# A fused two-block kernel: the RWKV stage with each head in its own half of the partitions

## The chip, the cores and the metric

The program runs on one core of one Trainium2 chip. A core has a matrix engine (TensorE, PE in the profile; its weight loads are PEld), three engines that work on vectors (VectorE or DVE, ScalarE or ACT, GpSimd or POOL), a queue engine that issues transfers (SyncE, SP), an on-chip memory of 128 partitions (SBUF), accumulators of 128 partitions (PSUM) and 16 DMA engines. The metric is the time of one execution on the device, in microseconds (us); less is better.

## The reference

Two transformer blocks follow each other over 512 tokens of 1024 channels, in float32: RWKV-7 in both directions beside neighbourhood attention, gated and projected; a mixture of experts; a second block of Hyena, gated linear attention and gated delta rule, and an MLP. The change touches the RWKV part, which has 8 heads of 64 channels:

```
r, k, v, ... = split(token_shift(h @ w_in))
kk = k * k_k;  kk = kk * rsqrt(sum(kk * kk, per head) + 1e-12)
step:  sa = S @ (-kk);  S = S * w + outer(sa, kk * a) + outer(v, k);  y = S @ r      # forward and backward in time
y = (y_f + y_b - mean) * rsqrt(var + eps) * lnx_g + lnx_b                            # per head
out = (y + sum(r * (k_f + k_b) * r_k, per head) * v) * g
```

## The kernel before, in words

The recurrence is computed in 8 chunks of 64 tokens. Two heads make a pair (128 partitions); 4 pairs times 2 directions are 8 units. For a unit, `dir_prep` (L487) makes decay factors (tiles cps to frho, fbet, falp), the scaled keys BK, the scaled queries EO, transposed copies (BKT, SV, VU) and the products of keys with keys (lps, L568), masked on DVE. `inverse` (L641) inverts the unit triangular matrix of each chunk and head: its 16x16 diagonal blocks go to DRAM and back so that each block lies on a partition of its own (L662, L664), are inverted by 15 steps of substitution on DVE (L671, L672), come back (L675, L677) and are combined by four rounds of 16 products of 64x64 (L692), which give TQ (L710). `scan` (L577) then goes through the chunks: xp (L585), copied to X, up = TQ X (L597), copied, sp (L603), and the next state on DVE (L605). The outputs yp (L613, L614) use states and values of all chunks. For the backward direction a group norm follows (L620 to L635), and `pair_prep` (L414) makes what a pair's two directions share.

In the code before, the two terms of a sum (state and value, say) are added by a product over all 128 partitions: the head's own half holds state and queries, the other half values and masked key products. So xp, sp and half of yp are products of 128 rows by 64 columns of the array, while up, the other half of yp and the inverse's products are 64 by 64.

A generator per activity writes the program down in turn (`weave`, L326): the next unit's preparation and inverse beside the present unit's scan, and all of this (weight 800) beside a filler (weight 170): gates and modulation rows (mps, L1227, from w_modb), then the projections of neighbourhood attention (`na_proj`: gpt, L319 to L321, then eight blocks gps with sums of squares, L735 to L741). A projection block is 24 products of 128x128 by 512 columns (gps, L288 to L290) with weights split on ACT and DVE (wh, wl). A scheduler of the framework then fixes the order on each engine when the program is built: it prefers what was written first among what it believes ready. At run time every engine goes through its list in order. A float32 product is two records on PE, one in float32r or a transpose is one.

Of the kernel before, what the change touches and what calls it, by code (L numbers as in the profile page):

```python
# [10 lines left out]
F32 = mybir.dt.float32  # L11
F32R = mybir.dt.float32r
I32 = mybir.dt.int32
AF = mybir.ActivationFunctionType
OP = mybir.AluOpType
# [10 lines left out]
# ---------------------------------------------------------------- constants (shapes alone)  # L26
def const_tables():
# [7 lines left out]
    c["bd16"] = np.tile(((s_[:, None] // 16) == (s_[None, :] // 16)).astype(np.float32), (2, 1))  # L35
# [41 lines left out]
def bias_table(rpb):  # L77
    """rpb [8, 15, 31] laid out per head and kind of column block as [128 queries, 256 keys], -1e30 out of the window"""
# [12 lines left out]
def blocks(w, cols):  # L91
    """w [1024, n] -> [len(cols), 128, 8, 128]: column blocks (-1: zeros), rows k*128 + p at [p, k]"""
# [9 lines left out]
def w2_cols():  # L102
    """column blocks of the second input projection: name -> list of 128 columns"""
# [41 lines left out]
def pad_heads(a):  # L145
    """[..., 192] -> [..., 256]: each head's 48 columns at a multiple of 64"""
# [27 lines left out]
class Tags:  # L174
    """a pool whose tags go by other names"""
# [8 lines left out]
class K:  # L184
# [8 lines left out]
    def view(self, tags, **kw):  # L193
        """the same kernel for a stream of its own: other PSUM tags, other pools"""
# [6 lines left out]
    # ---- constants  # L201
# [10 lines left out]
    def cvec(self, name, ap, n, pool=None):  # L212
        """A per-channel vector of n values as [128, n/128] columns."""
# [9 lines left out]
    # ---- 1/sqrt of a small tile, in place of x  # L223
# [20 lines left out]
        # the squares themselves go where the transposed parts will  # L244
# [27 lines left out]
    # ---- weights: raw load, exact split  # L272
# [2020 lines left out]
```

## Time and profile before

| | us |
|---|---|
| three runs | 2248.74, 2264.35, 2252.16 |
| median | 2252.16 |
| profiled execution, first to last instruction | 2259.9 |
| of these, until the last product of the RWKV stage's filler (L741) | 662.7 |
| PE busy / DVE busy / ACT busy / POOL busy, whole span | 2016.9 / 1253.3 / 725.8 / 314.7 |
| mean granted TensorE clock | 0.926 |

The profiled execution gives no time beside its span; the span is 7.7 us (0.3%) over the median and within the spread of the three runs. A busy PE is not a PE at its peak. Matmul records overlap, since they are pipelined, so what a product costs is read from start to start and not from its printed duration.

### The profile page before, as it was taken

How to read it: one execution, taken by the hardware profiler on the slowest of the kernel's cores; microseconds unless marked ns; L12 is line 12 of the kernel's file. 1: busy time of each engine (PE TensorE's matmuls, PEld its weight loads, DVE VectorE, ACT ScalarE, POOL GpSimd, SP SyncE). 2: the span in 40 equal slices, each digit the busy share in tenths (PEclk: the TensorE clock that was granted, in tenths of full speed). 3: DMA queues.
4: the chain of work that ended last, by engine and by line, in shares of the span. 5: the costliest groups of instructions: out<-in, count | busy, mean ns of one | idle time of the engine just before them, and what ended most of it. 6: DMA issues, size and time to landing. Idle time of an engine off the chain costs nothing. (4 is left out here: it accounts for less than half of the span.)

```text
span 2259.9 us, 34926 instructions
## 1 busy us (share of the span) xinstructions
PE 2016.9 (89%) x13608; PEld 1439.2 (64%) x13608; DVE 1253.3 (55%) x2742; ACT 725.8 (32%) x1422; POOL 314.7 (14%) x358
## 2 busy tenths in 40 slices
PE   7999999989968888989999487899989788999997
PEld 5666666657745675444534265676757477899897
DVE  4776777864326545554461487667447375433433
ACT  4332333222215433121322365423224125312321
POOL 0222222220110201102000031210001050000000
PEclk9999999998969998999999798998679899999998
DMA  5232221263267428897786532333113432222222
GB/s 150 99 107 80 66 88 55 76 204 114 92 209 230 143 87 297 294 346 244 297 309 225 192 112 86 101 113 106 38 47 132 162 112 94 93 94 94 94 94 75
DMA packets 183017, 319.25 MB, mean 141 GB/s; under 512 B 77896, under 2 KB 99160, under 8 KB 182842
## 3 DMA queue, kind: packets, MB, share of 16 engines
q1 hardware_dynamic: 175354, 303.28, 40.2%
q0 software_dynamic: 4608, 8.40, 1.1%
q10 hardware_dynamic: 2880, 5.24, 0.8%
q8 instruction: 109, 1.79, 0.3%
q14 instruction: 66, 0.54, 0.1%
HBM read 281.80 MB, written 43.44 MB: 144 GB/s over the span
## 5 line engine op out<-in xcount | busy, mean ns | idle before, releaser
L283 DVE TENSOR_TENSOR wl<-wraw,wh 128x1024 fp32r<-128x1024 f32 (+2 forms) x215 | 227.9, 1062 | 199.8 <-ACT wh L282 199.2
L282 ACT ACTIVATE wh<-wraw 128x1024 fp32r<-128x1024 f32 (+2 forms) x233 | 195.6, 844 | 274.2 <-PE gpt L321 145.1
L288 PE MATMUL gps<-hh,wh 128*128 128x512 f32 x568 | 236.3, 417 | 0.6 <-ACT wh L282 0.4
L290 PE MATMUL gps<-hl,wh 128*128 128x512 f32 x568 | 231.8, 409 | 0.0
L289 PE MATMUL gps<-hh,wl 128*128 128x512 f32 x568 | 231.6, 409 | 0.0
L1173 PE MATMUL hps<-w,xT 128*64 128x512 f32 x512 | 142.5, 610 | 3.4 <-DMA w<-in_w_moe 3.3
L320 PE MATMUL gpt<-wl,mh 128*128 128x256 f32 x512 | 142.9, 279 | 0.0
L319 PE MATMUL gpt<-wh,mh 128*128 128x256 f32 x512 | 142.9, 279 | 0.0
L321 PE MATMUL gpt<-wh,ml 128*128 128x256 f32 x512 | 142.9, 279 | 0.0
L288 PEld LDWEIGHTS gps<-hh,wh 128*128 128x128 f32 x568 | 108.4, 191 | 30.6 <-ACT st L765 1.4
L289 PEld LDWEIGHTS gps<-hh,wl 128*128 128x128 f32 x568 | 108.4, 191 | 24.2 <-issue 1.0
L290 PEld LDWEIGHTS gps<-hl,wh 128*128 128x128 f32 x568 | 107.9, 190 | 24.2 <-issue 0.7
L1999 POOL TENSOR_TENSOR x<-x,xev 128x512 f32<-128x512 f32 x36 | 49.9, 1392 | 407.9 <-DVE xev L1997 358.6
L289 PE MATMUL gps<-lhh,wl 128*128 128x512 f32 x232 | 96.4, 417 | 10.2 <-DVE wl L283 8.6
L288 PE MATMUL gps<-lhh,wh 128*128 128x512 f32 x232 | 96.2, 417 | 7.6 <-ACT cpad L1265 4.6
L319 PEld LDWEIGHTS gpt<-wh,mh 128*128 128x128 f32 x512 | 96.2, 188 | 0.1
L320 PEld LDWEIGHTS gpt<-wl,mh 128*128 128x128 f32 x512 | 96.2, 188 | 0.1
L321 PEld LDWEIGHTS gpt<-wh,ml 128*128 128x128 f32 x512 | 96.2, 188 | 0.0
L290 PE MATMUL gps<-lhl,wh 128*128 128x512 f32 x232 | 94.7, 410 | 0.2 <-DVE lhl L270 0.2
L1173 PEld LDWEIGHTS hps<-w,xT 128*64 128x64 f32 x512 | 37.1, 138 | 66.3 <-issue 51.2
L2015 DVE TENSOR_TENSOR uld<-uld 128x512 f32<-128x512 f32 x32 | 22.2, 692 | 88.1 <-ACT uld L2014 88.1
L319 PE MATMUL gpt<-wh,uh 128*128 128x256 f32 x224 | 66.0, 295 | 5.6 <-ACT wh L282 2.4
(1164 smaller groups left out, 4437.7 us busy)
## 6 DMA issues: line engine op xcount, KB each, us to landing
w<-in_w_moe SPq DMA_DIRECT2D x192, 512.0 KB
wraw<-in_w_modb SPq DMA_DIRECT2D x48, 512.0 KB
wraw<-in_w_in_2b SPq DMA_DIRECT2D x41, 512.0 KB
wraw<-in_w_inb SPq DMA_DIRECT2D x39, 512.0 KB
wraw<-in_w_mlp1b SPq DMA_DIRECT2D x32, 512.0 KB
wraw<-in_w_mlp2b SPq DMA_DIRECT2D x32, 512.0 KB
gd<-st SPq DMA_DIRECT2D x16, 256.0 KB
bm<-in_c_bias SPq DMA_DIRECT2D x16, 256.0 KB
```

The lines of the kernel that those rows point to most:

```text
L282: nc.scalar.activation(wh, raw[:, o:o + g], AF.Copy)
L283: self.we.tensor_sub(wl, raw[:, o:o + g], wh)
L288: nc.tensor.matmul(ps, wh, hh, start=first, stop=False)
L289: nc.tensor.matmul(ps, wl, hh, start=False, stop=False)
L290: nc.tensor.matmul(ps, wh, hl, start=False, stop=last)
L319: nc.tensor.matmul(ps, hh[:, g, sl], wh[:, k], start=f, stop=False, skip_group_check=True)
L320: nc.tensor.matmul(ps, hh[:, g, sl], wl[:, k], start=False, stop=False, skip_group_check=True)
L321: nc.tensor.matmul(ps, hl[:, g, sl], wh[:, k], start=False, stop=l, skip_group_check=True)
L1173: nc.tensor.matmul(ps[q], xT[:, 4 * kh + k, q], self.parts[h][:, 512 * (k - 2 * c):512 * (k - 2 * c) + 512], start=kh == 0 and k == 0, sto ...
L1999: (nc.gpsimd if last is None or cb < 3 else nc.vector).tensor_add(o, o, t)
L2015: nc.vector.tensor_mul(f, f, f)
```

## The change

Each head now stays in its own half of the partitions for both operands of every product, and the two terms of a sum are two products that accumulate in PSUM. BK becomes BE and KA, EO becomes AR with the masked products apart in PB and PK, and SV and VU become S, U and V. Elementwise operations that ran once per half run once over 128 partitions; the state scale no longer needs POOL; the copy of up is one ACT operation. Beta, kappa and values are transposed by products of 64x64 with the identity. Both norms take their root on [128, 4, 2] values and are spread again by ACT and four products (`over_norm`) in place of a root and a reciprocal over [128, 512]. The inverse gets its diagonal blocks by a mask of their own (nd16) straight from PSUM and its other blocks from PB. The gated delta rule's inverse keeps its operations (`in_parts`). In the diff, docstrings and comments are left out.

```diff
     blk[:64, :64] = 1.0
     blk[64:, 64:] = 1.0
     c["blk"] = blk
-    c["bd16"] = np.tile(((s_[:, None] // 16) == (s_[None, :] // 16)).astype(np.float32), (2, 1))
+    up, same = s_[:, None] < s_[None, :], lambda n: (s_[:, None] // n) == (s_[None, :] // n)
+    two = lambda a: np.tile(a.astype(np.float32), (2, 1))
+    c["bd16"] = two(same(16))
+    c["nd16"] = two(up & same(16))
+    far = up & ~same(16)
+    c["pm"] = two(np.concatenate([far, s_[:, None] <= s_[None, :]], 1))
...
-                TQ, = yield from self.inverse([U["N"]], d)
+                TQ, = yield from self.inverse([(U["Nd"], lambda q, P=U["PB"]: P[q, :, 0, :])], d)
...
+    def over_norm(self, sq, pool, eps, scale, name):
+        nc, C = self.nc, self.C
+        ps = self.ps.tile([128, 4, 2], F32, name=name + "s", tag="p", bufs=2)
+        for tt in range(4):
+            nc.tensor.matmul(ps[:, tt], sq[:, tt * 128:(tt + 1) * 128], C["blk"][:, ::64], start=True, stop=True)
+        r = pool.tile([128, 4, 2], F32, name=name + "r")
+        nc.scalar.activation(r, ps, AF.Sqrt, bias=eps, scale=scale)
+        nc.vector.reciprocal(r, r)
+        R = pool.tile([128, 4, 2, 64], F32, name=name + "b", tag="rs")
+        nc.scalar.activation(R, r[:, :, :, None].to_broadcast([128, 4, 2, 64]), AF.Copy)
+        ps = self.ps.tile([128, 512], F32, name=name + "p", tag="p", bufs=2)
+        for tt in range(4):
+            nc.tensor.matmul(ps[:, tt * 128:(tt + 1) * 128], R[:, tt].rearrange("p h c -> p (h c)"), C["ident"], start=True, stop=True)
+        return ps
...
         kk = pt.tile([128, T], F32, name="kk")
         sq = pt.tile([128, T], F32, name="sq", tag="sq")
         nc.scalar.activation(sq, kS, AF.Square, scale=self.kkv[:, hp:hp + 1])
...
+        ps = self.over_norm(sq, pt, self.eps12, 1.0, "kn")
...
         frho, fbet, falp = fac
-        BK = pt.tile([128, 8, 2, 64], F32, name="BK")
+        BE, KA = [pt.tile([128, 8, 64], F32, name=n) for n in ("BE", "KA")]
         b = self.rt.tile([128, T], F32, name="bb", tag="sq")
+        tm = lambda ap: nat(ap).rearrange("p (c t) -> p c t", t=64)
         nc.vector.scalar_tensor_tensor(b, a, 1.0, kk, op0=OP.add, op1=OP.mult)
...
+        nc.vector.scalar_tensor_tensor(BE, tm(b), 0.5, fbet, op0=OP.mult, op1=OP.mult)
+        nc.gpsimd.tensor_mul(KA, tm(kd), fbet)
+        AR = rp.tile([128, 8, 2, 64], F32, name=f"AR{d}")
+        nc.vector.tensor_mul(AR[:, :, 0, :], tm(kk), falp)
+        nc.vector.tensor_mul(AR[:, :, 1, :], tm(rS), frho)
         Dc = rp.tile([128, 8], F32, name=f"Dc{d}")
         nc.vector.reciprocal(Dc[:, :7], falp[:, 1:, 0])
         nc.vector.tensor_mul(Dc[:, :7], Dc[:, :7], frho[:, :7, 63])
...
         if d:
-            vr = self.rt.tile([128, T + 64], F32, name="vr", tag="rs")
-            nc.vector.tensor_copy(vr[:, 64:], vS[:, 64:][:, ::-1])
-            nc.gpsimd.memset(vr[:, :64], 0.0)
+            vr = self.rt.tile([128, T], F32, name="vr", tag="rs")
+            nc.vector.tensor_copy(vr, vS[:, ::-1])
         else:
             vr = vS
...
+        tok = []
+        for n, x in (("BT", BE), ("KT", KA), ("V", vr.rearrange("p (c t) -> p c t", t=64))):
+            ps = ps_.tile([128, 8, 64], F32, name="tps", tag="p", bufs=2)
+            for c in range(8):
+                for q in hq:
+                    nc.tensor.matmul(ps[q, c], x[q, c], C["ident"][q, q], start=True, stop=True)
+            o = rp.tile([128, 8, 64], F32, name=f"{n}{d}")
+            nc.scalar.activation(o, ps, AF.Copy)
+            tok.append(o)
+        Nd = pt.tile([128, 8, 64], F32, name=f"Nd{d}")
+        PB, PK = [rp.tile([128, 8, 2, 64], F32, name=f"{n}{d}") for n in ("PB", "PK")]
         for g in range(2):
-            for h in range(2):
-                q, o = slice(64 * h, 64 * h + 64), slice(64 - 64 * h, 128 - 64 * h)
+            sl = slice(4 * g, 4 * g + 4)
+            for x, o, m in ((BE, PB, "pm"), (KA, PK, "mask")):
                 ps = ps_.tile([128, 4, 128], F32, name="lps", tag="p", bufs=2)
                 for c in range(4):
...
+                    for q in hq:
+                        nc.tensor.matmul(ps[q, c, :], x[q, 4 * g + c], AR[q, 4 * g + c].rearrange("p a t -> p (a t)"), start=True, stop=True)
+                if x is BE:
+                    nc.vector.tensor_mul(Nd[:, sl], ps[:, :, :64], C["nd16"][:, None, :].to_broadcast([128, 4, 64]))
+                nc.vector.tensor_mul(o[:, sl].rearrange("p c a t -> p c (a t)"), ps, C[m][:, None, :].to_broadcast([128, 4, 128]))
+        return dict(Nd=Nd, PB=PB, PK=PK, AR=AR, Dc=Dc, tok=tok)
...
         nc, C, ps_, pt = self.nc, self.C, self.ps, self.rd
-        EO, SV, VU, BKT, Dc = U["EO"], U["SV"], U["VU"], U["BKT"], U["Dc"]
+        AR, PB, PK, Dc = U["AR"], U["PB"], U["PK"], U["Dc"]
+        BT, KT, V = U["tok"]
         hq = [slice(64 * h, 64 * h + 64) for h in range(2)]
+        S = self.rp.tile([128, 8, 64], F32, name=f"S{d}")
+        Us = self.rp.tile([128, 8, 64], F32, name=f"U{d}")
         for c in range(8):
             xp = ps_.tile([128, 64], F32, name="xp", tag="s", bufs=2)
-            for h, q in enumerate(hq):
-                nc.tensor.matmul(xp[q], EO[h][:, c, 0, :], SV[h][:, c, :], start=True, stop=True)
+            for q in hq:
+                nc.tensor.matmul(xp[q], PK[q, c, 0, :], V[q, c, :], start=True, stop=c == 0)
+            if c:
+                for q in hq:
+                    nc.tensor.matmul(xp[q], AR[q, c, 0, :], S[q, c, :], start=False, stop=True)
             X = pt.tile([128, 64], F32, name="X", bufs=2)
             nc.vector.tensor_copy(X, xp)
-            if c < 7:
+            if 0 < c < 7:
                 SD = pt.tile([128, 64], F32, name="SD", bufs=2)
-                for h, q in enumerate(hq):
-                    if h:
-                        nc.gpsimd.tensor_scalar(SD[q], SV[h][q, c, :], Dc[q, c:c + 1], None, op0=OP.mult)
-                    else:
-                        nc.scalar.activation(SD[q], SV[h][q, c, :], AF.Copy, scale=Dc[q, c:c + 1])
+                nc.scalar.activation(SD, S[:, c, :], AF.Copy, scale=Dc[:, c:c + 1])
             up = ps_.tile([128, 64], F32, name="up", tag="s", bufs=2)
-            for h, q in enumerate(hq):
+            for q in hq:
                 nc.tensor.matmul(up[q], TQ[q, c, :], X[q], start=True, stop=True)
-            nc.scalar.activation(VU[0][hq[0], c, :], up[hq[0]], AF.Copy)
-            nc.vector.tensor_copy(VU[1][hq[1], c, :], up[hq[1]])
+            nc.scalar.activation(Us[:, c, :], up, AF.Copy)
             if c < 7:
                 sp = ps_.tile([128, 64], F32, name="sp", tag="s", bufs=2)
-                for h, q in enumerate(hq):
-                    nc.tensor.matmul(sp[q], BKT[:, c, h, :], VU[h][:, c, :], start=True, stop=True)
-                for h, q in enumerate(hq):
-                    nc.vector.scalar_tensor_tensor(SV[h][q, c + 1, :], sp[q], Dc[q, c:c + 1], SD[q], op0=OP.mult, op1=OP.add)
+                for q in hq:
+                    nc.tensor.matmul(sp[q], KT[q, c, :], V[q, c, :], start=True, stop=False)
+                for q in hq:
+                    nc.tensor.matmul(sp[q], BT[q, c, :], Us[q, c, :], start=False, stop=True)
+                if c:
+                    nc.vector.scalar_tensor_tensor(S[:, c + 1, :], sp, Dc[:, c:c + 1], SD, op0=OP.mult, op1=OP.add)
+                else:
+                    nc.vector.tensor_scalar(S[:, 1, :], sp, Dc[:, 0:1], None, op0=OP.mult)
             yield 2.5
         if d == 0:
             self.y = self.ry.tile([128, T], F32, name="y")
         y = self.y
         yp = ps_.tile([128, 8, 64], F32, name="yp", tag="i", bufs=2)
         for c in range(8):
-            for h, q in enumerate(hq):
-                nc.tensor.matmul(yp[q, c, :], SV[h][:, c, :], EO[h][:, c, 1, :], start=True, stop=False)
-                nc.tensor.matmul(yp[q, c, :], VU[h][q, c, :], U["MB"][q, c, :], start=False, stop=True)
+            for q in hq:
+                nc.tensor.matmul(yp[q, c, :], V[q, c, :], PK[q, c, 1, :], start=True, stop=False)
+            if c:
+                for q in hq:
+                    nc.tensor.matmul(yp[q, c, :], S[q, c, :], AR[q, c, 1, :], start=False, stop=False)
+            for q in hq:
+                nc.tensor.matmul(yp[q, c, :], Us[q, c, :], PB[q, c, 1, :], start=False, stop=True)
         ypf = yp.rearrange("p c t -> p (c t)")
         if d == 0:
             nc.scalar.activation(y, ypf, AF.Copy)
         nc.vector.tensor_add(y, ypf[:, ::-1], y)
...
-        ps = ps_.tile([128, 512], F32, name="vps", tag="p", bufs=2)
-        nc.tensor.matmul(ps, C["blk"], sq, start=True, stop=True)
-        nc.scalar.activation(sq, ps, AF.Sqrt, bias=self.epsgn, scale=1.0 / 64)
-        nc.vector.reciprocal(sq, sq)
-        nc.vector.scalar_tensor_tensor(y, y, self.lng[:, hp:hp + 1], sq, op0=OP.mult, op1=OP.mult)
+        ps = self.over_norm(sq, pt, self.epsgn, 1.0 / 64, "yn")
+        nc.vector.scalar_tensor_tensor(y, y, self.lng[:, hp:hp + 1], ps, op0=OP.mult, op1=OP.mult)
         nc.vector.scalar_tensor_tensor(y, y, self.lnb[:, hp:hp + 1], bo, op0=OP.add, op1=OP.add)
         nc.gpsimd.tensor_mul(y, y, P["gt"])
         nc.sync.dma_start(self.yad[hp * 128:(hp + 1) * 128, :], y)
...
         fb = self.rib
         F = pt.tile([128, nz, 8, 16], F32, name="F16", bufs=fb)
...
+        for z, (Nd, _) in enumerate(Ns):
+            nc.vector.tensor_reduce(F[:, z], Nd.rearrange("p u (b t) -> p u t b", b=4), axis=AX.X, op=OP.add)
...
+                    nc.tensor.matmul(ps[q, u, :], lhs(q)[:, u, :], rhs[q, u, :], start=True, stop=True)
         Z, W = [], list(Qd)
         for z in range(nz):
-            ps = mm(No[z], Vd[z])
-            Z.append(pt.tile([128, 8, 64], F32, name="Z", tag="zw", bufs=2 * nz))
+            ps = mm(Ns[z][1], Vd[z])
+            Z.append(pt.tile([128, 8, 64], F32, name="Z", tag="zw", bufs=2))
             nc.scalar.activation(Z[z], ps, AF.Copy, scale=-1.0)
         for i in range(2):
             for z in range(nz):
-                ps = mm(Z[z], W[z])
+                ps = mm(lambda q, z=z: Z[z][q], W[z])
                 W[z] = pt.tile([128, 8, 64], F32, name="W", tag="zx", bufs=2)
                 nc.vector.tensor_add(W[z], ps, Qd[z])
         TQ = []
         for z in range(nz):
-            ps = mm(Z[z], W[z])
+            ps = mm(lambda q, z=z: Z[z][q], W[z])
             t = self.rp.tile([128, 8, 64], F32, name=f"TQ{key + z}")
             if neg:
                 nc.vector.scalar_tensor_tensor(t, ps, -1.0, Qd[z], op0=OP.mult, op1=OP.subtract)
...
+    def in_parts(self, pool, N):
+        w, o = [pool.tile([128, 8, 64], F32, name=n, tag=t, bufs=2) for n, t in (("Nw", "zw"), ("No", "No"))]
+        self.nc.vector.tensor_mul(w, N, self.C["bd16"][:, None, :].to_broadcast([128, 8, 64]))
+        self.nc.gpsimd.tensor_sub(o, N, w)
+        return w, lambda q: o[q]
...
-            TQ = yield from self.inverse([N[:, e] for e in range(2)], 2 * key, neg=False)
+            TQ = yield from self.inverse([self.in_parts(self.ri, N[:, e]) for e in range(2)], 2 * key, neg=False)
-            t, = yield from self.inverse([N.rearrange("p e s t -> p (e s) t")], neg=False)
+            t, = yield from self.inverse([self.in_parts(self.ri, N.rearrange("p e s t -> p (e s) t"))], neg=False)
```

Behind the RWKV stage and its filler the order of every engine is the same in both programs. Counted over the built order up to the last L741 (L738 in the change), PE goes through 782 stretches of products of one array shape (rows by columns) before, and 412 after.

The first place is PE in the middle of a unit, one chunk of the scan beside projection products. Before:

```order
L597 MATMUL up<-X,TQ_3211 64x64 x2
L288 MATMUL gps<-hh,wh 128x512
L289 MATMUL gps<-hh,wl 128x512
L603 MATMUL sp<-VU_2767,BKT_2752 64x64
L614 MATMUL yp<-MB_2791,VU_2767 64x64
L603 MATMUL sp<-VU_2768,BKT_2752 64x64
L613 MATMUL yp<-EO_2744,SV_2766 64x64
L614 MATMUL yp<-MB_2791,VU_2768 64x64
L290 MATMUL gps<-hl,wh 128x512
L288 MATMUL gps<-hh,wh 128x512
L289 MATMUL gps<-hh,wl 128x512
L585 MATMUL xp<-SV_2765,EO_2743 64x64
```

The same place in the change:

```order
L589 MATMUL up<-X,TQ_2171 64x64 x2
L594 MATMUL sp<-V_1709,KT_1690 64x64 x2
L293 MATMUL gps<-hh,wh 128x512
L596 MATMUL sp<-U_2340,BT_1671 64x64 x2
L578 MATMUL xp<-V_1709,PK_1713 64x64 x2
L294 MATMUL gps<-hh,wl 128x512
L295 MATMUL gps<-hl,wh 128x512
L581 MATMUL xp<-S_2339,AR_1648 64x64 x2
```

Single products of alternating shapes have become pairs of one shape (x2: one product for each head), and fewer projection products stand between the steps of the chain up, sp, xp.

The second place is SP behind the last unit, where the stores qkd and vd and the loads vb and bm of the next stage meet. Before:

```order
L277 DMA wraw<-in_w_inb 128x1024
L775 DMA qg<-in_q_gain 64x1 x2
L775 DMA qg<-in_k_gain 64x1 x2
L782 DMA vb<-vd 128x1x512 x8
L787 DMA qkx<-qkd 128x512
L806 DMA bm<-in_c_bias 128x2x256 x2
L636 DMA yad<-y 128x512
L736 DMA qkd<-st 128x512 x2
```

In the change:

```order
L772 DMA qg<-in_k_gain 64x1 x2
L803 DMA bm<-in_c_bias 128x2x256 x2
L632 DMA yad<-y 128x512
L282 DMA wraw<-in_w_inb 128x1024
L1132 DMA w<-in_w_moe 128x1024
L282 DMA wraw<-in_w_inb 128x1024
L724 DMA vd<-st 128x2x256
L1132 DMA w<-in_w_moe 128x1024
L724 DMA vd<-st 128x2x256
L779 DMA vb<-vd 128x1x512 x8
L733 DMA qkd<-st 128x512
```

The eight vb loads stand ahead of the first qkd store now, behind the last vd stores, and more of the filler comes after the last norm: 181 products of `na_proj` before (153 gps, 28 ssp) and 330 in the change (192 gps, 106 gpt, 32 ssp).

## Rows read from the trace of the kernel before

**Rows 1.** Busy time by stretch (us): PE, PEld, DVE, ACT, POOL, granted clock, DMA share, GB/s.

```profile
0.00:120.00 120.00, 100.43 (x504) 75.77 (x504) 79.25 (x157) 47.34 (x72) 16.94 (x26) 0.97 0.43 131
120.00:420.00 300.00, 293.82 (x2306) 194.38 (x2308) 218.07 (x499) 98.65 (x194) 68.68 (x85) 1.00 0.24 73
420.00:545.00 125.00, 113.53 (x1065) 71.54 (x1057) 85.79 (x201) 30.45 (x69) 23.14 (x32) 0.92 0.48 156
545.00:662.70 117.70, 98.36 (x667) 77.21 (x665) 31.03 (x58) 23.65 (x41) 14.74 (x16) 0.90 0.39 126
470.00:520.00 50.00, 43.14 (x428) 25.15 (x427) 31.98 (x61) 11.32 (x24) 10.20 (x12) 0.86 0.58 193
```

**Rows 2.** Timeline of PE: start, us, line, tiles, array rows*columns, shape, records.

```profile
239.95 0.39 PE L288 MATMUL gps<-hh,wh 128*128 128x512 f32 x1
240.18 0.40 PE L289 MATMUL gps<-hh,wl 128*128 128x512 f32 x1
240.50 1.15 PE L692 MATMUL ips<-W,Z 64*64 64x64 f32 x32
241.58 1.09 PE L530 MATMUL tps<-ct,BK 128*128 128x128 f32 x8
242.43 0.48 PE L290 MATMUL gps<-hl,wh 128*128 128x512 f32 x1
...
251.16 1.16 PE L568 MATMUL lps<-EO,BK 64*128 64x128 f32 x8
...
257.66 0.40 PE L288 MATMUL gps<-hh,wh 128*128 128x512 f32 x1
257.98 0.33 PE L597 MATMUL up<-X,TQ 64*64 64x64 f32 x4
258.25 0.50 PE L289 MATMUL gps<-hh,wl 128*128 128x512 f32 x1
258.58 0.40 PE L290 MATMUL gps<-hl,wh 128*128 128x512 f32 x1
258.91 0.33 PE L603 MATMUL sp<-VU,BKT 128*64 128x64 f32 x2
259.17 0.33 PE L614 MATMUL yp<-MB,VU 64*64 64x64 f32 x2
259.42 0.33 PE L613 MATMUL yp<-EO,SV 128*64 128x64 f32 x2
259.68 0.50 PE L288 MATMUL gps<-hh,wh 128*128 128x512 f32 x1
```

**Rows 3.** Timeline of PE near the end of the last scan, same columns.

```profile
565.38 0.28 PE L321 MATMUL gpt<-wh,hl 128*128 128x256 f32 x1
565.50 0.28 PE L319 MATMUL gpt<-wh,hh 128*128 128x256 f32 x1
```

**Rows 4.** Timeline of PE at the sums of squares, same columns.

```profile
600.66 1.05 PE L741 MATMUL ssp<-ct,st 128*128 128x2 f32 x8 [0.50 <-POOL st L738]
```

**Rows 5.** Timeline of one unit from its first product to TQ, PE.

```profile
231.73 1.05 PE L498 MATMUL cps<-ct,sw 128*128 128x128 f32 x8
...
299.94 1.05 PE L498 MATMUL cps<-ct,sw 128*128 128x128 f32 x8
```

**Rows 6.** The same unit on SP and DVE.

```profile
258.36 0.37 SPq L662 DMA_DIRECT2D nd<-F  x1
...
291.92 0.62 SPq L675 DMA_DIRECT2D qd<-q  x1
...
311.86 0.69 DVE L710 SCALAR_TENSOR_TENSOR TQ<-ips,qv 128x512 f32<-128x512 f32 x1 [0.17 <-PE ips L692]
```

**Rows 7.** Timeline of SP and PE behind the last unit.

```profile
608.28 14.62 SPq L782 DMA_DIRECT2D vb<-vd  x8
...
629.31 1.35 SPq L736 DMA_DIRECT2D qkd<-st  x2
...
639.26 1.01 PE L741 MATMUL ssp<-ct,st 128*128 128x2 f32 x4 [15.56 <-POOL st L738]
```

More of the change, by code (lines that the diff above doesn't have):

```diff
@@ L433, in pair_prep @@
         yield 5
-        self.shifted(self.proj1(8 + hp), 8 + hp, vS[:, 64:])
+        self.shifted(self.proj1(8 + hp), 8 + hp, vS)
         yield 5
@@ L490, in dir_prep @@
         kk, a, kd, rS, vS = P["kk"], P["aa"][d], P["kd"][d], P["rS"], P["vS"]
+        hq = [slice(64 * h, 64 * h + 64) for h in range(2)]
         nat = (lambda ap: ap[:, ::-1]) if d else (lambda ap: ap)
@@ L524, in dir_prep @@
         nc.vector.tensor_mul(Dc[:, :7], Dc[:, :7], frho[:, :7, 63])
-        BKT = rp.tile([128, 8, 2, 64], F32, name=f"BKT{d}")
-        for g in range(2):
-            ps = ps_.tile([128, 4, 128], F32, name="tps", tag="p", bufs=2)
-            for c in range(4):
-                nc.tensor.transpose(ps[:, c, :], BK[:, 4 * g + c].rearrange("p a t -> p (a t)"), C["ident"])
-            nc.scalar.activation(BKT[:, 4 * g:4 * g + 4].rearrange("p c a t -> p c (a t)"), ps, AF.Copy)
         if d:
-            vr = self.rt.tile([128, T + 64], F32, name="vr", tag="rs")
-            nc.vector.tensor_copy(vr[:, 64:], vS[:, 64:][:, ::-1])
-            nc.gpsimd.memset(vr[:, :64], 0.0)
+            vr = self.rt.tile([128, T], F32, name="vr", tag="rs")
@@ L537, in dir_prep @@
+            nc.vector.tensor_copy(vr, vS[:, ::-1])
         else:
             vr = vS
-        SV = [rp.tile([128, 8, 64], F32, name=f"SV{h}{d}") for h in range(2)]
-        VU = [rp.tile([128, 8, 64], F32, name=f"VU{h}{d}") for h in range(2)]
-        for g in range(3):
-            n = min(4, 9 - 4 * g)
-            ps = ps_.tile([128, 4, 128], F32, name="vps", tag="p", bufs=2)
-            for c in range(n):
-                j = 4 * g + c
-                m = 128 if j < 8 else 64
-                nc.tensor.transpose(ps[:m, c, :], vr[:, 64 * j:64 * j + m], C["ident"])
-            j0 = 4 * g
-            lo, hi = max(j0, 1), j0 + n
-            nc.scalar.activation(SV[1][:64, lo - 1:hi - 1, :], ps[:64, lo - j0:n, 64:], AF.Copy)
-            hi = min(j0 + n, 8)
-            if hi > j0:
-                nc.scalar.activation(SV[0][64:, j0:hi, :], ps[64:, :hi - j0, :64], AF.Copy)
@@ L555, in dir_prep @@
-        for h in range(2):
-            o = slice(64 - 64 * h, 128 - 64 * h)
-            nc.gpsimd.tensor_copy(VU[h][o], SV[h][o])
-            nc.gpsimd.memset(SV[h][64 * h:64 * h + 64, 0, :], 0.0)
-        N = pt.tile([128, 8, 64], F32, name=f"N{d}")
-        MB = rp.tile([128, 8, 64], F32, name=f"MB{d}")
+        tok = []
[7 more added lines that the diff above has]
+            tok.append(o)
@@ L562, in dir_prep @@
+        Nd = pt.tile([128, 8, 64], F32, name=f"Nd{d}")
+        PB, PK = [rp.tile([128, 8, 2, 64], F32, name=f"{n}{d}") for n in ("PB", "PK")]
         for g in range(2):
-            for h in range(2):
-                q, o = slice(64 * h, 64 * h + 64), slice(64 - 64 * h, 128 - 64 * h)
+            sl = slice(4 * g, 4 * g + 4)
+            for x, o, m in ((BE, PB, "pm"), (KA, PK, "mask")):
                 ps = ps_.tile([128, 4, 128], F32, name="lps", tag="p", bufs=2)
                 for c in range(4):
-                    cc = 4 * g + c
-                    nc.tensor.matmul(ps[:, c, :], BK[q, cc].rearrange("p a t -> p (a t)"),
-                                     EO[h][q, cc].rearrange("p a t -> p (a t)"), start=True, stop=True)
-                sl = slice(4 * g, 4 * g + 4)
-                mk = C["mask"][:, None, :].to_broadcast([128, 4, 128])
-                nc.vector.tensor_mul(EO[h][o, sl].rearrange("p c a t -> p c (a t)"), ps[o], mk[o])
-                nc.vector.tensor_mul(N[q, sl], ps[q, :, :64], mk[q, :, :64])
-                nc.vector.tensor_mul(MB[q, sl], ps[q, :, 64:], mk[q, :, 64:])
@@ L628, in scan @@
         nc.scalar.activation(sq, y, AF.Square)
-        ps = ps_.tile([128, 512], F32, name="vps", tag="p", bufs=2)
-        nc.tensor.matmul(ps, C["blk"], sq, start=True, stop=True)
-        nc.scalar.activation(sq, ps, AF.Sqrt, bias=self.epsgn, scale=1.0 / 64)
-        nc.vector.reciprocal(sq, sq)
-        nc.vector.scalar_tensor_tensor(y, y, self.lng[:, hp:hp + 1], sq, op0=OP.mult, op1=OP.mult)
+        ps = self.over_norm(sq, pt, self.epsgn, 1.0 / 64, "yn")
+        nc.vector.scalar_tensor_tensor(y, y, self.lng[:, hp:hp + 1], ps, op0=OP.mult, op1=OP.mult)
         nc.vector.scalar_tensor_tensor(y, y, self.lnb[:, hp:hp + 1], bo, op0=OP.add, op1=OP.add)
@@ L691, in mm @@
                     q = slice(64 * h, 64 * h + 64)
-                    nc.tensor.matmul(ps[q, u, :], lhs[q, u, :], rhs[q, u, :], start=True, stop=True)
+                    nc.tensor.matmul(ps[q, u, :], lhs(q)[:, u, :], rhs[q, u, :], start=True, stop=True)
             return ps
```

29 lines of the change are left out of this document (3 added, 26 removed).

## The prediction, made before the change was run

> **What bounds the kernel now.** I read the busy time by stretch first, since the change touches nothing behind 662.7 us of the 2259.9 us span, and asked who is busy there [rows 1]. From 120 to 420 us TensorE is busy 293.82 of 300 us at a granted clock of 1.00, DVE 218, ACT 99, POOL 69, and the DMA share is 0.24. So six of the eight units run at TensorE's own pace: what leaves its list shortens the span, and what leaves another engine's list does not. The other stretches are looser: PE is idle 19.6 us of the first 120, 11.5 of 420 to 545, 19.3 of the rest. From 470 to 520 the clock is 0.86, between its levels of 1.2 and 2.4 GHz, with DMA at 0.58 and 193 GB/s, while the loads of w_modb run. Behind the last unit one wait of 15.56 us stands out: the sums of squares wait for a square on POOL, which waits for the store qkd, and on SP that store (629.31) is behind eight vb loads of 14.62 us in all [rows 7].
>
> The next view is TensorE's timeline, read from start to start [rows 2]. A 512-column product costs 0.23 us beside its like (239.95 to 240.18) and 0.32 to 0.33 when the next product has another array shape. The pair up costs 0.27, and 16 products of 64x64 (8 pairs, L692) 1.08. So a further pair costs (1.08 - 0.27) / 7 = 0.116 and a stretch of its own about 0.15 on top. Lone products of sp or yp cost 0.25 to 0.26 each, more than a pair in a row. What a change of shape costs is thus the price that this change plays on.
>
> **The change part by part, on TensorE.** The stretches of one array shape are counted in the built order, the prices are those of the timeline.
>
> - Changes of shape: 782 stretches become 412, so 370 fewer at 0.156 on average (0.14 to 0.20 by shape; the rows give 0.15 for 64x64 and about 0.10 on each side of a lone 512-column product). That is **-57.8**.
> - Transposes: 136 of 128x128 at 0.11 (8 took 0.85, 241.58 to 242.43) are 15.0; now 3 x 8 x 8 = 192 pairs of 64x64 at 0.117 are 22.5: **+7.5**.
> - lps: 128 products of one head each become 128 pairs. Four took at most 1.16 [rows 2], some 0.22 each with 0.19 for the stretch, and a pair overlaps as the others do: about **+2**.
> - Norms: eight blk products of 512 float32 columns go, each about 0.86 (an estimate: cps, four products of 128 columns in the same type, takes 1.05 with its tail [rows 5]). Eight times four products of two columns come, 1.05 for four with their tail [rows 4], and four of 128 columns. With 0.9 for each four that is 8 x (0.9 + 0.9 - 0.86) = 7.5: **+7.4**, as counted.
> - Scan: 624 products, mostly lone, become 944 in 472 pairs. Without the changes of shape, 624 cost 57.5; 472 x 0.117 = 55.2, and 57.1 with the stretches' first products: **-0.4**. Accumulating in PSUM is new and no row shows its price. The nearest rows are yp, where the second product of a sum already accumulates, at 0.26 to the first one's 0.25: so I take nothing. Above I allow half a pair more, 0.06 on some 350 accumulating pairs (+21); below, nothing, since adding to a sum takes no columns away.
> - The filler's and the other small products stand in fuller groups in the new order: **-5.6**.
>
> The sum on TensorE is -57.8 + 7.5 + 2 + 7.4 - 0.4 - 5.6, some **-46** us, 583 becoming 537. What stands beside these 583 us before, up to 662.7, is 79 us of start, waits and lower clock; the start is the same.
>
> **The other engines.** DVE loses about 105 us over the stage (two large reciprocals of the norms, half of the state's operations, half of the masking), POOL about 65, ACT a little. I cost them at nothing: TensorE covers them today. If TensorE were no longer the bound, they would be what helps the units to keep up. The mask reduction of the diagonal blocks moves ahead of the inverse. SP has as many issues as before; the added constants (98 KB) load at the start beside the weights.
>
> **Waits that are new.** Three places, each bounded from both sides.
>
> - In the scan, between up and sp stood three 512-column products or two (257.98 to 258.91, about 0.65 of cover for the copy of up), and now it is one (0.33). Over 64 chunks that uncovers up to 64 x 0.5 = 32 us and at least nothing, since the second term of a sum alone needs the copy and the first one (KT with V, PK with V) needs none. I take 8, nearer to nothing, as the copy is one ACT operation and pairs of other chunks stand between.
> - The w_modb loads: 28 of 0.52 MB are 14.7 MB. At the 193 GB/s of 470 to 520 [rows 1] they take 76 us. The PE work they now stand beside is about 56 us by the same prices. So 0 to 20 more; I take 10, since the queue also reaches more than that mean.
> - Behind the last norm more filler is left: 39 gps at 0.23, 106 gpt at 0.12 [rows 3] and 4 sums make 22.7 us more there, and as much less beside the units. It is in the sum already. The vb loads still stand ahead of qkd on SP, so the stall stays, with a little more work before it: 12 for 15.6, -3. The bounds are -15.6 (gone) and 0.
>
> Together +15 us (from -16 to +46, where all is given back). The sum is -46 + 15 = **-31**. Against the profiled execution (2259.9, 7.7 over the median of 2252.2) that is 2229; against the runs' median **2221**.
>
> **Rivals.**
>
> *The unit's own chain becomes the bound, in part.* A unit goes from its first product at 231.73 to TQ at 311.86, 80 us, of which the trip to DRAM, the substitution and the way back take 258.36 to 291.92, 33.6 us [rows 5, 6]. The next unit starts 68.2 us after it. The substitution stays. The PE work in the units' region is, by the sum, 486 / 8 = 61 us a unit before and 415 / 8 = 52 after. If chain and loads give back half to two thirds, the saving is 10 to 20 us: **2235 to 2258**, say 2245. For it: less filler beside the units, DMA at 0.58. Against: DVE and POOL operations leave the same chain, and the stretch of 300 us shows 6 us of idle.
>
> *The chain bounds in full.* This is the case on the slower side. If a unit cannot come sooner than the 68 us of today, nothing is saved in the region, and the 22.7 us of filler that were cover there are paid behind the last norm: 2252 + 23 = **2275**. It decides when chain plus issue of a unit stays over 61 us; I reckon 43 to 52 with the shorter elementwise work, so it is unlikely.
>
> *Pairs don't overlap.* If the two heads' products, in different halves of the rows, had to follow each other, 664 pairs would cost 0.117 more and the 128 of lps 0.22 more: 78 + 28 = 106, and with the waits then covered 2252 - 46 + 106 = **2312**. Rows speak against: L692 writes both halves of one accumulator and takes 1.08 for 16 products, where singles would make some 2.0 [rows 2]. The Trainium skill, page "TensorEngine Tiling (Array Packing)", section "Gotcha 1: PSUM Pressure", says "Different row tiles cannot access same PSUM bank simultaneously". By that rule these pairs would be serial; the trace, at 0.116 a pair, doesn't agree, unless the accumulating form behaves otherwise.
>
> *Waits shrink too.* With the 15.6 us stall gone and no new wait the time is 2252 - 46 - 15, some **2190**, to 2200 with a few us of new waits.
>
> **How the numbers follow.** Chances: forecast (2200 to 2235) 0.55; chain in part 0.22; chain in full 0.07; serial pairs 0.04; waits shrink 0.12. Less than 1% (22.5 us) can't be told from no change. Under 2229.7 lie four fifths of the forecast, the waits that shrink, and little of the second case: 0.59. Over 2274.7 lie the serial pairs and half of the full chain: 0.09. Within 1% is 0.32. The range 2188 to 2260 leaves out the slower cases and half of the lowest.
>
> **What would show it.** In the changed profile the stretch up to the last sum of squares (L738) should end near 632 instead of 662.7, with the units 55 to 60 us apart. Pairs of sp, xp, yp at 0.12 each in a row, and 0.27 alone, show the main step right; at 0.2 and more the pairs are serial. PE's waits should be about 15 us more in all, on the copies of up and X, and on mps during the w_modb loads. DVE should fall to some 310 us in the stage with no effect of its own. If PE's idle time from 120 to 400 us exceeds 30 us, the unit's chain is the bound and the forecast is wrong; if the sums on the later stages, whose orders are the same, differ by more than a few us, the cause lies outside this account.

## The result, and the profile after

| | before | change |
|---|---|---|
| median of the first runs (us) | 2258.26 of 4 | 2227.06 of 4 |
| ratio, 95% interval | | 0.9868 [0.9824, 0.9911] |
| in a later comparison (us) | 2251.65 of 11 | 2227.85 of 6 |
| ratio, 95% interval | | 0.9881 [0.9844, 0.9917] |
| first profile: span / end of the last sum of squares (us) | 2259.9 / 662.7 | 2229.7 / 640.7 |
| second profile: the same (us) | 2244.2 / 657.3 | 2236.4 / 636.6 |

The change is 1.2 to 1.3% faster, by 24 to 31 us between medians. In either pair of profiles the stage that it touches is 21 to 22 us shorter.

The busy time by stretch of the change answers to [rows 1], in the same columns.

```profile
0.00:120.00 120.00, 102.19 (x751) 79.81 (x752) 68.24 (x158) 47.38 (x67) 6.80 (x11) 1.00 0.49 134
120.00:420.00 300.00, 291.67 (x3625) 214.70 (x3623) 173.64 (x396) 101.14 (x191) 28.31 (x22) 1.00 0.27 77
420.00:545.00 125.00, 109.20 (x1445) 74.40 (x1442) 48.25 (x137) 26.38 (x61) 7.39 (x4) 0.81 0.50 147
545.00:640.80 95.80, 73.04 (x391) 61.60 (x390) 15.06 (x23) 17.47 (x25) 9.62 (x9) 0.89 0.51 164
```

TensorE still fills the 300 us (8.3 us idle for 6.2), with 174 us of DVE for 218 and 28 of POOL for 69. What is new is the third row: the granted clock from 420 to 545 us is 0.81, where it was 0.92.

The timeline of TensorE in the middle of a scan answers to [rows 2].

```profile
246.17 0.33 PE L596 MATMUL sp<-U,BT 64*64 64x64 f32 x4
246.34 0.28 PE L578 MATMUL xp<-V,PK 64*64 64x64 f32 x4
246.46 0.28 PE L613 MATMUL yp<-PB,U 64*64 64x64 f32 x4
246.57 0.28 PE L608 MATMUL yp<-PK,V 64*64 64x64 f32 x4
246.78 0.51 PE L293 MATMUL gps<-hh,wh 128*128 128x512 f32 x1
247.22 0.33 PE L581 MATMUL xp<-S,AR 64*64 64x64 f32 x4
247.38 0.28 PE L611 MATMUL yp<-AR,S 64*64 64x64 f32 x4
247.60 0.51 PE L294 MATMUL gps<-hh,wl 128*128 128x512 f32 x1
```

A pair in a row costs 0.11 to 0.12 us (246.34, 246.46, 246.57), accumulating ones too. Four pairs take 0.61 us where single products took 0.25 to 0.26 each. A lone 512-column product between pairs takes 0.44 (246.78 to 247.22): 0.23 is the price of such a product beside its like [rows 2], and the other 0.21 is that of two changes of shape.

The tail, first on SP and then on TensorE, answers to [rows 7].

```profile
567.31 13.42 SPq L779 DMA_DIRECT2D vb<-vd  x8
581.16 2.10 SPq L733 DMA_DIRECT2D qkd<-st  x1
...
593.23 0.33 SPq L784 DMA_DIRECT2D qkx<-qkd  x1
...
594.53 1.87 PE L738 MATMUL ssp<-ct,st 128*128 128x2 f32 x8 [15.37 <-POOL st L735]
```

The stall is as long as before, 15.37 us for 15.56.

### The profile page after: what moved, and what is told of

It is laid out like the page before. It is cut to its first block, busy times and chain, and to the rows that moved or that the text cites. A ratio compares the mean times of both kernels' runs of the same rounds, so it can differ in the third digit from the quotient of the medians.

```text
span 2229.7 us, 37859 instructions
## 1 busy us (share of the span) xinstructions
PE 1979.0 (89%) x15280; PEld 1445.7 (65%) x15280; DVE 1141.5 (51%) x2542; ACT 718.0 (32%) x1390; POOL 241.8 (11%) x246
## 5 line engine op out<-in xcount | busy, mean ns | idle before, releaser
L288 DVE TENSOR_TENSOR wl<-wraw,wh 128x1024 fp32r<-128x1024 f32 (+2 forms) x215 | 223.3, 1040 | 202.8 <-ACT wh L287 202.3
L1271 DVE SCALAR_TENSOR_TENSOR cout<-cpad,cw,cout 128x512 f32<-128x512 f32 (+1 forms) x90 | 68.6, 762 | 2.0
```

The source lines that it names most:

```text
L288: self.we.tensor_sub(wl, raw[:, o:o + g], wh)
L1271: nc.vector.scalar_tensor_tensor(ov[:n], pv[:n, :, j:j + L], wcol[:n, j:j + 1], ov[:n], op0=OP.mult, op1=OP.add)
```

## The experiments

Stage end is the end of the last sum of squares, and last norm the start of the last product that spreads or sums a norm, both from the profile; ratios are to the kernel before.

| kernel | median us | ratio, 95% interval | last unit starts | last norm | stage end |
|---|---|---|---|---|---|
| before, profiles 1, 2 | 2251.65 | | 479.5, 479.1 | 596.1, 592.6 | 662.7, 657.3 |
| change, profiles 1, 2 | 2227.85 | 0.9881 [0.9844, 0.9917] | 442.6, 441.8 | 548.1, 544.3 | 640.7, 636.6 |
| wide_values | 2268.38 | 1.0079 [1.0050, 1.0109] | 470.6 | 581.8 | 673.3 |
| old_norms | 2199.34 | 0.9790 [0.9756, 0.9825] | 429.5 | 512.3 | 606.8 |
| old_kn | 2212.01 | 0.9829 [0.9793, 0.9866] | 442.8 | 530.0 | 615.3 |
| old_yn | 2206.82 | 0.9830 [0.9779, 0.9881] | 435.2 | 520.5 | 610.9 |
| deep_st | 2221.53 | 0.9861 [0.9827, 0.9895] | 442.1 | 545.0 | 629.9 |
| store_by_act | 2221.50 | 0.9869 [0.9834, 0.9905] | 444.1 | 546.8 | 634.8 |
| store_by_act_old_norms | 2194.33 | 0.9767 [0.9732, 0.9803] | 430.3 | 513.0 | 606.9 |
| even_mods | 2230.32 | 0.9903 [0.9868, 0.9939] | 460.8 | 549.0 | 644.6 |
| st_and_mods | 2226.04 | 0.9874 [0.9840, 0.9909] | 467.3 | 555.4 | 647.2 |
| st_mods_norms | 2199.96 | 0.9778 [0.9749, 0.9807] | 438.3 | 520.6 | 607.9 |

### The same two kernels again

> The kernel before, unchanged, for a second profile. In the first pair of profiles 22 us of the 30 us between the spans lie before the last sum of squares, and 8 us between 1600 and 1625 us of the kernel before, where the order of all engines is the same in both kernels but the granted clock stayed at 0.61 before and was 0.99 in the change. Theory: the 8 us belong to the execution, not to the change; then the clock of that stretch differs between executions of one kernel, and here it may as well return early (span then about 2252). Rival: the change causes it (other timing of loads into that stretch); then this profile repeats 0.55 to 0.65 from 1580 to 1625.

> The changed kernel, unchanged, timed in five rounds and with a second profile. If the stage alone brings the gain, the ratio is 0.990 (22 of 2255 us); if the 8 us of the later stretch belong to the change, it is 0.9865. The stage should end at 640 +- 3 us; the clock of 1575 to 1593 us may be 0.55 or 1.0 by the first theory, and is about 1.0 by the second.

No edit. Two rows each of the change's first profile, of its second, and of the first and the second of the kernel before, in windows of 20 us (columns as in [rows 1]), in the later stretch whose order no kernel changes:

```profile
1560.00:1580.00 20.00, 20.00 (x128) 14.25 (x127) 9.12 (x35) 5.67 (x14) 0.00 (x0) 0.69 0.16 53
1580.00:1600.00 20.00, 20.00 (x145) 14.95 (x146) 9.86 (x34) 4.91 (x14) 3.32 (x4) 0.83 0.12 40
```

```profile
1560.00:1580.00 20.00, 20.00 (x132) 14.36 (x132) 8.95 (x34) 6.44 (x16) 0.00 (x0) 0.67 0.12 43
1580.00:1600.00 20.00, 20.00 (x94) 13.30 (x95) 6.90 (x25) 2.64 (x7) 2.49 (x3) 0.50 0.07 24
```

```profile
1580.00:1600.00 20.00, 20.00 (x103) 14.88 (x103) 7.34 (x30) 5.22 (x13) 0.00 (x0) 0.53 0.16 50
1600.00:1620.00 20.00, 20.00 (x121) 13.72 (x119) 7.96 (x29) 4.77 (x13) 1.77 (x2) 0.64 0.09 31
```

```profile
1580.00:1600.00 20.00, 20.00 (x145) 14.43 (x144) 9.88 (x39) 6.35 (x16) 0.00 (x0) 0.76 0.13 45
1600.00:1620.00 20.00, 20.00 (x147) 14.52 (x146) 10.35 (x36) 4.95 (x13) 4.04 (x5) 0.83 0.12 40
```

The second profile of the change stays at half clock (0.50) where the first rose (0.83), and the second of the kernel before rises (0.83) where its first stayed low (0.64). From the stage's end to that of the span the change took 1589.0 and 1599.8 us, the kernel before 1597.2 and 1586.9. So the first theory holds, as far as two profiles of each can show it: these 8 us belong to the execution, and what the change brings is the 21 to 22 us of the stage. The interval of the timed ratio (19 to 35 us of 2251.65) takes that in.

### The price of a change of shape

```diff
...
+                o = rp.tile([128, 2, 8, 64], F32, name=f"{n}{d}")
...
-                nc.tensor.matmul(xp[q], PK[q, c, 0, :], V[q, c, :], start=True, stop=c == 0)
+                nc.tensor.matmul(xp[q], PK[:, c, 0, :], V[:, h, c, :], start=True, stop=c == 0)
```

V holds zeros in the other head's half, set by POOL, and each head's values are copied to their place by an ACT operation of their own; sp and yp are changed in the same way.

> The changed kernel with its three value terms (xp, sp and yp) as products of 128 rows by 64 columns again: values with zeros in the other head's half, all rows of PK and KT. The products stay as many and stay pairs (two column halves); what changes is the number of stretches of one array shape up to the last sum of squares: 412 become 686. Theory (a change of shape costs 0.14 to 0.20 us and TensorE is the bound): TensorE's list grows by 41 us and the stage ends 30 to 41 us later, the time 1.3 to 1.8% longer. Rival (the gain came from fewer vector operations or from the units' chain): under 10 us.

TensorE's timeline of this kernel in a scan:

```profile
257.91 0.33 PE L595 MATMUL up<-X,TQ 64*64 64x64 f32 x4
258.17 0.34 PE L600 MATMUL sp<-V,KT 128*64 128x64 f32 x4
258.44 0.49 PE L295 MATMUL gps<-hl,wh 128*128 128x512 f32 x1
258.86 0.33 PE L602 MATMUL sp<-U,BT 64*64 64x64 f32 x4
259.12 0.34 PE L584 MATMUL xp<-V,PK 128*64 128x64 f32 x4
259.39 0.33 PE L619 MATMUL yp<-PB,U 64*64 64x64 f32 x4
259.65 0.34 PE L614 MATMUL yp<-PK,V 128*64 128x64 f32 x4
259.91 0.50 PE L293 MATMUL gps<-hh,wh 128*128 128x512 f32 x1
```

The sequence sp, xp, yp, yp is that of 246.17 in the change. There the pairs followed each other at 0.12 us, here at 0.26 or 0.27, although each is still a pair. The stage ends 33 to 37 us later (expected 30 to 41). The time is 40.5 us longer between medians, some 45 by the ratios (expected 29 to 40). The edit also gives ACT and POOL some 5 and 7 us more to do, but the time is TensorE's: it is busy for 611.6 us up to the stage's end, where the change has 576.0 and 574.8. The theory holds, and with it the kind of the term of -57.8 us; its size comes out at 0.8 to 0.9 of what was reckoned.

### The norms

```diff
-        ps = self.ps.tile([128, 4, 2], F32, name=name + "s", tag="p", bufs=2)
...
         ps = self.ps.tile([128, 512], F32, name=name + "p", tag="p", bufs=2)
...
-        return ps
+        nc.tensor.matmul(ps, C["blk"], sq, start=True, stop=True)
+        nc.scalar.activation(sq, ps, AF.Sqrt, bias=eps, scale=scale)
+        nc.vector.reciprocal(sq, sq)
+        return sq
```

> The changed kernel with both norms as before: one product with blk over 512 columns, root and reciprocal over 128x512 (the reciprocal took 3.35 us of DVE each). TensorE's list gets 5.8 us shorter, DVE's some 27 us longer, in 8 pieces on the units' chains. Theory (TensorE bounds, DVE's savings are worth nothing): the stage ends 0 to 6 us earlier. Rival (the vector work on the chain matters): it ends 10 to 27 us later.

The first theory had the direction and was far off in size, the rival had neither: the stage ends 30 to 34 us earlier, the time is 28.5 us shorter between medians, 20 by the ratios. Most of it lies in the last unit. From its start to the last norm the change takes 105.5 and 102.5 us, and with the old norms 82.8. So 20 to 23 of the 30 to 34 us are there. The next two kernels take the norms apart, by `if name == "kn":` (or `"yn"`) before the line for ps and the four new ones.

> The changed kernel with the norm of the keys (kn) alone as before; four norms of yn stay compact. TensorE's list is 1.4 us shorter. With both norms as before the stage ended 30 to 34 us earlier, of which 5.8 are TensorE's list and about 18 the stretch of the last scan, which ran at a granted clock of 0.50 from 508 to 538 us in both profiles of the change and at 1.00 there. Theory 1 (the compact norm is a longer chain through four engines and holds back each unit): kn stands at the head of every pair, so half or more of the 28 us comes back. Theory 2 (mainly the clock of the last scan, which the order there decides): the time goes by whether the stretch from 500 to 545 is at 0.5 or 1.0, by 15 to 20 us, and otherwise by under 8.

> The changed kernel with the norm of the outputs (yn) alone as before. TensorE's list is 3.8 us shorter. Theory 1: little comes back, under 8 us, since yn stands at the end of a pair. Theory 2: as for kn, 15 to 20 us if the last scan is at full clock, else under 8.

Windows of 6 us around the last unit's scan (columns as in [rows 1]), first of the second profile of the change, then of the kernel with the old norm of yn:

```profile
484.00:490.00 6.00, 2.85 (x24) 0.40 (x16) 0.00 (x0) 0.00 (x0) 0.00 (x0) 0.50 0.91 237
496.00:502.00 6.00, 5.47 (x109) 3.41 (x106) 2.07 (x3) 0.61 (x1) 0.00 (x0) 0.94 0.78 242
502.00:508.00 6.00, 3.65 (x54) 2.80 (x54) 3.36 (x7) 3.19 (x8) 0.00 (x0) 0.91 0.80 221
508.00:514.00 6.00, 6.00 (x50) 4.63 (x50) 0.73 (x3) 0.57 (x2) 0.00 (x0) 0.50 0.19 67
526.00:532.00 6.00, 6.00 (x50) 4.66 (x49) 0.73 (x3) 0.22 (x1) 0.00 (x0) 0.50 0.00 0
538.00:544.00 6.00, 6.00 (x52) 5.92 (x52) 1.85 (x3) 4.25 (x6) 0.00 (x0) 1.00 0.34 113
```

```profile
484.00:490.00 6.00, 5.08 (x72) 3.27 (x74) 0.69 (x1) 0.60 (x1) 1.52 (x1) 0.52 0.83 263
496.00:502.00 6.00, 5.35 (x89) 3.69 (x83) 3.42 (x8) 3.96 (x9) 0.00 (x0) 1.00 0.76 231
502.00:508.00 6.00, 6.00 (x95) 4.80 (x94) 1.26 (x6) 1.14 (x4) 0.00 (x0) 1.00 0.44 137
508.00:514.00 6.00, 6.00 (x93) 4.62 (x87) 1.25 (x5) 1.14 (x4) 0.00 (x0) 1.00 0.01 3
```

In both kernels the loads of w_modb stop TensorE near 484 us and the clock falls to its lower level. In the change TensorE is idle once more, 2.35 of 6 us from 502 to 508, and from 508 to about 537 the clock stays at 0.50, though TensorE is busy all the time. With the old yn that second gap is missing and the scan runs at 1.00, 93 records in 6 us for 50. Most of the gap in the change's first profile is a wait of one product of the modulation rows:

```profile
504.44 0.28 PE L594 MATMUL sp<-V,KT 64*64 64x64 f32 x4
506.81 0.33 PE L1231 MATMUL mcp<-ct,st 128*128 128x128 f32 x1 [2.09 <-ACT st L1228]
507.07 0.33 PE L596 MATMUL sp<-U,BT 64*64 64x64 f32 x4
```

The copy st that it waits for stands on ACT, first in that profile of the change and then with the old yn:

```profile
505.22 1.06 ACT L287 ACTIVATE wh<-wraw 128x1024 fp32r<-128x1024 f32 x1 [7.71 <-DMA wraw<-in_w_vb]
506.18 0.58 ACT L1228 ACTIVATE st<-mps 128x512 f32<-128x512 f32 x1
```

```profile
496.43 0.60 ACT L1234 ACTIVATE st<-mps 128x512 f32<-128x512 f32 x1 [7.80 <-PE mps L1230]
497.11 1.06 ACT L287 ACTIVATE wh<-wraw 128x1024 fp32r<-128x1024 f32 x1
```

In the change the copy is behind a split of weights that waits 7.71 us for the load of w_vb, which shares SP's queue with w_modb. With either norm or both as before, the built order has the copy ahead of the split, and the product waits 0.33 us or nothing.

What the lower clock costs there can be read from one chunk of the scan, from one sp to the next, with the same eight pairs and six products of gpt: in the change at 0.50, with the old kn at 1.00.

```profile
510.57 0.48 PE L596 MATMUL sp<-U,BT 64*64 64x64 f32 x4
515.04 0.48 PE L596 MATMUL sp<-U,BT 64*64 64x64 f32 x4
```

```profile
505.69 0.33 PE L602 MATMUL sp<-U,BT 64*64 64x64 f32 x4
508.35 0.33 PE L602 MATMUL sp<-U,BT 64*64 64x64 f32 x4
```

That is 4.47 us for 2.66. By this price the 31 to 34 us at 0.50, from 507 to 537.7 and 541.5 us in the two profiles, cost 12 to 14 us (an estimate).

Theory 2 fits better: either norm alone brings the clock of the scan back, and 15 to 20 us of the last unit with it (102.5 to 105.5 us becomes 87.2 and 85.3). Theory 1 had expected under 8 us from yn; the medians say 21, the ratios 11. Not all is the clock: with both norms old the last unit also starts 12 to 13 us earlier, of which TensorE's list explains at most 6. And that the second gap is what holds the clock down was not tried by itself. Five profiles (the change twice, deep_st, store_by_act, wide_values) had that gap of over 2 us of 6, with the copy behind the split and the scan behind the gap, and all five had the long stretch at 0.50. In all five the clock returned a few us after the last pair of the scan, when only products over the whole array ran (at 541.5 and 537.7 us in the change). The four with an old norm and the loads where they were had neither the gap nor the stretch. The kernel before had the gap (3.57 and 3.79 of 6 busy) and was low for some 6 to 16 us only; even_mods and st_and_mods had waits of 3.4 and 2.8 us with 512-column products behind them, and were low for some 7 and 10 us. So the gap alone doesn't decide.

### The stall behind the last unit

```diff
-            f = st.tile([128, T], F32, name="st", bufs=2)
+            f = st.tile([128, T], F32, name="st", bufs=4)
```

(and so wherever the tag st is used.)

> The changed kernel with four buffers of st for two, so that the projection blocks behind the last unit need not wait for the store qkd that stands behind the eight vb loads on SP; the order of the products is the same. Theory: the waits of the sums of squares (22.7 us, the longest 15.4) are on the path and fall to 8 or less, so the stage ends 13 to 16 us earlier (about 625) and the time falls by 10 to 16 us. Rival: the vb loads and qkd stores are needed by the attention that follows anyway, so the end moves little and the time by under 5.

The wait only moved on by one block:

```profile
591.10 1.87 PE L738 MATMUL ssp<-ct,st 128*128 128x2 f32 x8 [12.09 <-POOL st L735]
```

The stage ended 7 to 11 us earlier and the medians differ by 6.3 us, inside the intervals. Theory half right: the wait is on the path, but two more blocks of buffers don't cover it.

```diff
-            nc.sync.dma_start(self.qkd[j], f)
+            nc.scalar.dma_start(self.qkd[j], f)
```

> The changed kernel with the stores qkd issued by ACT, right behind the copy that makes their data, and so not behind the vb and qkx loads on SP. Four st buffers took only 3 us off the longest wait of the sums of squares (15.4 to 12.1). Theory: the store then lands in about 3 us, the long wait falls to under 4 us, the stage ends 11 to 15 us earlier and the time falls by as much. Rival: the store is late because the transfers themselves queue behind the vb loads (SP issues it at 581 us, and the load that needs it is let go at 593), whichever engine issues it; then the wait stays over 10 us.

> The same with both norms as before, the fastest candidate. If the gains add: 2199 less 11 to 15 us, about 2187. If the transfers queue: 2199.

The longest wait of the sums of squares fell from 15.4 to 5.2 us in the first (expected under 4) and 2.0 in the second, but the stage ended only 2 to 6 us earlier in the first and not earlier in the second; the medians are 6.4 and 5.0 us lower, inside the intervals. SP and TensorE of the second:

```profile
532.39 14.50 SPq L772 DMA_DIRECT2D vb<-vd  x8
547.00 0.97 SPq L282 DMA_DIRECT2D wraw<-in_w_inb  x1
```

```profile
565.19 0.79 PE L294 MATMUL gps<-hh,wl 128*128 128x512 f32 x1 [13.94 <-DVE wl L288]
```

The wait took another name. The next weights stand behind the same eight vb loads on SP, and the product that needs them waits 13.94 us. Neither theory named it: moving one victim out of the way of the vb loads exposes the next. That their time on SP's queue is the whole of the stall is not shown. In old_kn and old_yn the same eight loads stand in two groups of four and take 4.9 and 5.4 us of the queue in all, and the sums of squares still wait 12.5 and 12.7 us. The store itself is slow to land there: in the change the POOL operation that needs it starts 12.3 us after its issue (581.16 to 593.44), in old_kn 10.4 (551.67 to 562.10). What the transfers wait for stays open.

### The loads of w_modb, spread

```diff
-                    yield from self.weave((self.gates(), 80), (self.mods(), 20))
+                    yield from self.weave((self.gates(), 80), (self.mods(), 55))
```

> The changed kernel with the modulation rows spread evenly over the filler (weight 55 for 20), so that the w_modb loads lie beside all units and not in 420 to 505 us. Theory: in that stretch the loads make TensorE wait (some 25 us of idle and waiting between 420 and 510) and the granted clock fall to 0.57 to 0.83 from 440 to 545; spread, the clock stays near 1.0 there and the stage ends 15 to 25 us earlier. Rival: what is saved there is lost as waits of the units for weights, whose buffers and queue the loads share: under 5 us.

> Both edits together: four st buffers and the modulation rows spread evenly. If the two costs are apart, the gains add: the time falls by 20 to 40 us against the change, the stage ends near 605. If they share a cause, the sum is that of the larger.

> The same with the old norms too. By the first theory 5 to 10 us less than with the new norms (TensorE's list is 526 us for 536); by the rival 10 us or more longer.

The clock from 440 to 545 us rose from 0.77 to 0.93, as expected, and yet the stage ended 4 to 8 us later. The rival fits better. The last unit now starts 18 to 19 us later, and the waits of TensorE from 60 to 545 us are headed by another line:

```profile
PE gps L293 <- ACT wh L287: 10.2, 4, 4.4
PE mps L1224 <- DMA wraw<-in_w_modb: 8.3, 5, 2.6
```

In the change the first of these lines is not among the waits of that window, and the second has 8.8 us. Three of the four waits in that first line, 6.8 us, lie ahead of the last unit's start, so some 7 of the 18 to 19 us are waits for weights; the rest was not taken apart. With deeper st buffers the time didn't fall either (2226.04, where 20 to 40 us less than the change were expected if the gains add). With the old norms besides it is 2199.96, 26 us less and not the 5 to 10 expected, and the same as old_norms alone: the gain there is that of the norms.

**The fastest.** old_norms, st_mods_norms and store_by_act_old_norms have overlapping intervals, at 0.977 to 0.979 of the kernel before. All three are faster than the change. The old norms alone are the simplest edit, 2.1% below the kernel before.

## Why the prediction held, and where it missed

**TensorE's list (-46) was right in kind and too large.** Pairs in a row cost the 0.117 us taken for them, accumulating or not, and 274 more changes of shape cost 33 to 37 us of stage for 41 reckoned. By that the term of -57.8 was mis-sized: some 46 to 52 us. Up to the stage's end TensorE was busy for 606.1 us before and 576.0 in the change, 600.0 and 574.8 in the second profiles. With what ran at the lower clock reckoned at the higher one (an estimate from windows of 2 us, priced as the chunk above or at one half) its list got 36 to 40 us shorter, so 6 to 10 of the 46 were missing. 120 to 420 us stayed TensorE's, with 8.3 us idle. The last five units start 56 us apart in the mean (217.5 to 442.6 in four steps) where 62 stood before, as forecast, though unevenly.

**Serial pairs: no.** The rival's rule, from the Trainium skill's page "TensorEngine Tiling (Array Packing)", section "Gotcha 1: PSUM Pressure", doesn't agree with these rows: two heads write both halves of one accumulator at 0.12 us a pair, also when they add to it.

**The chain as the bound: no.** TensorE's idle time from 120 to 400 us is 7.9 us, under the 30 that would have spoken for it.

**The other engines at nothing.** DVE is at 304 us up to 632, as forecast. That its relief brings nothing is borne out by the norms: with the old ones DVE was busy for 326.8 us up to the stage's end instead of 305.2, in a faster kernel and not a slower one.

**The new waits (+15) came out near in sum and wrong in kind.** The stage is 21 to 22 us shorter; with 36 to 40 off the list, some 15 to 19 were given back, inside the bounds of -16 and +46. Of the three places, the copies of up and X, put at +8, gave nothing back: TensorE's waits on them were 4.1 us before and are 0.6 and 2.0. The waits on w_modb grew by 4 to 5 us (4.1 and 4.0 before, 8.8 and 8.0 now) for the +10. The stall of the tail was priced at 12 us and stayed at 15.4. The missing step is the clock of the last scan, a term that the prediction did not have: it said nothing of what a gap does to the clock behind it. That is some 30 us at half clock, 12 to 14 us by the chunk's price, for 6 to 16 us at half clock before. Together the stage ended at 640.7 and 636.6, not at 632.

**The norms (+7.4) were mis-sized most.** As a term of TensorE's list it was about right: 5.8 after regrouping, and some 7 to 11 us by the same estimate from the profiles. As what the compact norms cost the kernel it was not: undoing them gave 20 to 28 us. The prediction costed each part of the change on TensorE's list alone, and did not ask what the part does to the order around the loose stretch. There it put a copy of ACT's behind a wait for weights, and the scan behind that gap of 2 us ran at half clock.

**The agreement of 2227 with 2221** is closer than the steps were, and in part luck: the stage gave 21 to 22 us of the 31, and the rest of the first medians is of the size by which executions differ in the later stretch.

**Small slips.** The terms of the list add up to -46.9, the chance over 2274.7 to 0.075 and not 0.09. And in [rows 2] the accumulating yp (L614) takes 0.25 us and the first one (L613) 0.26, not the other way round. Nothing hangs on these.

## What to carry to other kernels

Where small products of several array shapes alternate on a full TensorE, count the stretches of one shape in the built order and price them from start to start. Here that gave 41 us for an undo that cost 33 to 37, and 46 for a change that took 36 to 40 off the list. Then price each part of the change once more by undoing it alone: one that looked like 7 us of the bill was 20 to 28, and in its profiles a gap of 2 us came with some 30 us at half clock. And before buying buffers or queues against a stall, find what the late transfer waits for: otherwise the stall takes the next name.

## What the runs showed of the hardware

The granted clock stayed at 0.50 for about 30 us while TensorE was shown busy in every us of it, with pairs of 64x64 and products of 256 columns, in five profiles; the same kind of work ran at 1.00 where no gap came just before. The Trainium skill's page "TensorE: Matmul & The Clock Gate", Part 1, says that "the default state is throttled, and activity releases the throttle"; these rows do not contradict that, but a stream that the profile shows as fully busy did not release it here. In all five the clock came back a few us after the scan's last pair, behind products over the whole array alone; what decides was not tried. Eight loads of 128 rows by 2 KB took 12.3 to 14.6 us of SP's queue in the eleven profiles in which they stood together, the two of the kernel before among them, and 4.9 to 6.3 us in the three in which they stood in two groups of four (old_kn, old_yn, st_mods_norms).
